# A mixture-of-experts stage whose TensorE order is written out by hand

## The chip, the cores and the metric

The kernel runs on one core of a Trainium2 chip. The metric is the device time of one execution in microseconds (us). TensorE is PE (PEld its weight loads), VectorE DVE, ScalarE ACT, GpSimd POOL, and SyncE, which issues the loads, SP.

## The reference, cut to what matters

Two layers of a diffusion transformer over 256 tokens of width 1024. Each layer mixes tokens (convolution, gated delta rule, windowed attention) and then channels. The second layer's channel mixer, the last stage of the kernel, is a mixture of eight experts, two for each token:

```python
top_logit, top_e = lax.top_k(logits, TOP_K)          # TOP_K = 2
gates = jax.nn.softmax(top_logit, axis=-1)
...
xb = h[row_tok]                                      # the tokens of each expert
y  = (silu(xb @ w_gate[e]) * (xb @ w_up[e])) @ w_down[e]     # 1024 -> 3584 -> 1024
out = segment_sum(y * row_gate, row_tok)
```

All is float32. `h` is the normalized x, scaled and shifted by a modulation.

## The kernel before

The change touches the routine `lean`, which runs when the experts' token counts fit fixed capacities: CAPS = [64, 96, 64, 160, 64, 96, 96, 32] tokens, the experts sorted so that the counts fit; this is the branch that runs. The other branch (`SEQ`) is not executed.

**Units and slots.** Each expert's 3584 inner columns are seven units of 512 (q = 0 to 6). A unit has three slots: gate (k = 0), up (k = 1) and down (k = 2). The matrix part of a slot is 2 MB, in four loads of 512 KB. `UNITS` lists experts 0, 1, 2 and 5 one after the other, then 3 and 7 alternating by q, then 6 and 4. `LEAN` lists the slots in the order of the program. With b the next unit and a the one before it, that order is gate(b), down(a), up(b).

**Loads.** The loads go into a ring of 36 buffers named r (nine slots), all issued by SP at L1186 (`ring_load`) in the order of the slots; load u waits until PE is done with load u - 36.

**Three ways of multiplying.** For 64 or 32 tokens (kind "f") PE does float32 matmuls, with tokens in parts of the columns of the array: L1535 for gate and up, L1769 for down. For 96 tokens (kind "t"), L1649 and L1652, and L1681 and L1684. Expert 3 has 160 tokens, a block of 128 (kind "s") and a rest of 32 (kind "f"). In the block of 128 each piece of weights, 128 x 512, is split in two parts, whi by ACT (L1499) and wlo = r - whi by DVE, or by POOL for every fourth piece (L1501, `wpiece`; four buffers of whi, three of wlo), and three matmuls use them (`three`, L1507 to L1509); the third, on wlo, is held back until after the first two of the next piece. A slot of that block has eight pieces.

**Between up and down.** `act` is Silu by ACT (L1729) and the product with up by DVE (L1730). `turn` transposes the result on PE (L1738; L1662 for 96 tokens) and copies it to hT, of which there is one buffer (DVE, L1745), or for expert 3 splits it into hr (ACT, L437) and hl (DVE, L438). The inner function `late` calls the former unit's turn in the middle of a gate.

**Gather, scatter, combine.** `lean_gather` brings the tokens of the next experts together: a one-hot matrix oe (DVE, L1614), products with the tokens on PE (L1623, two matmuls each, shown as four records), and a modulation out of PSUM by ACT (L433) or DVE (L431). It is a generator: each `next(steps)` in the program does one bank of PSUM. `BATCHES` says where it starts: experts 1 and 2 (width 160) and 5 and 4 (160), then 3, 7 and 6 (288). Expert 0 (width 64) is gathered ahead of the stage. `scatter` makes the matrix that puts an expert's rows back: DVE writes two halves into a buffer of hT (L1446), PE transposes them (L1450), ACT copies them (L1452). At q = 6 the results are copied to ys (`lean_rows`, L1696) and multiplied by the scatter matrix (`lean_combine`, L1717).

**What sets the order.** The program is written in the order above, but a scheduler of the framework decides the order of instructions on every engine, PE's too, by its own estimates of when operands are ready. PSUM has eight banks: four of tag x (gate, up, turn, gather, scatter, combine) and four of tag y (down).

Of the kernel before, what the change touches and what calls it, by code (L numbers as in the profile page):

```python
# [22 lines left out]
KT = 8  # L23
# [144 lines left out]
class Build:  # L168
# [995 lines left out]
    def ring_fill(self, n):  # L1164

        for _ in range(n):
# [4 lines left out]
    SEQ = [(0, 0), (1, 0)] + [t for q in range(6) for t in ((0, q + 1), (2, q), (1, q + 1))] + [(2, 6)]  # L1171
# [3 lines left out]
            + [(u[0], k, u[1]) for a, b in zip(UNITS, UNITS[1:]) for k, u in ((0, b), (2, a), (1, b))]  # L1175
# [195 lines left out]
    def expert(self, e, blocks):  # L1371
# [13 lines left out]
        hs, up, tr = {}, {}, {}  # L1385
        self.rest = None
        ahead = self.gather(e + 1) if e + 1 < NE else iter(())
        for j, (k, q) in enumerate(self.SEQ):
# [14 lines left out]
            else:  # L1403
                if q == 6:
                    next(ahead, None)
                for bi in order:
                    if bi in hs:
                        tr[bi] = self.turn(hs[bi], blocks[bi][2])
                if q == 6:
                    next(ahead, None)  # L1410
                for bi in order:
                    self.down(w, tr[bi], blocks[bi][1], blocks[bi][2], q, py[bi])
# [105 lines left out]
    def up(self, w, x, m, split, late):  # L1518

        nc = self.nc  # L1520
        if split:
            out = self.ps()
            for k in range(KT):
                if k == 4:
                    late()
# [5 lines left out]
        for k in range(KT):  # L1531
            if k == 4:
                late()
# [6 lines left out]
    def lean(self, first):  # L1540
# [5 lines left out]
        up = {}  # L1546
        for i, (e, k, q) in enumerate(self.LEAN):
            if (e, k, q) in self.BATCHES:
                got, steps = self.lean_gather(*self.BATCHES[e, k, q])
                xs.update(got)  # L1550
            w, x = self.slot(i), xs[e]
            bl = x["blocks"]
            if k == 0:
# [6 lines left out]
                up = [self.lean_up(w, b, late if b is bl[-1] else lambda: None) for b in bl]  # L1560
            elif k == 1:
                pu = [self.lean_up(w, b, lambda: None) for b in bl]
                pend = x, [self.act(g, u) for g, u in zip(up, pu)]
                if done:
                    self.lean_combine(done)
                    done = None
                if q == 6:
                    x["ogt"] = [self.scatter(e, s0, m, j) for j, (s0, m, _, _) in enumerate(bl)]
                next(steps, None)
            else:  # L1570
                if q == 0:
                    x["py"] = [[self.ps("y") for _ in range(1 if kind == "f" else 2)] for _, _, kind, _ in bl]
                if pend:
                    late()
                for b, h, py in zip(bl, x["tr"], x["py"]):
                    self.lean_down(w, h, b, q, py)
                if q == 6:
# [58 lines left out]
    def lean_up(self, w, b, late):  # L1636
# [7 lines left out]
        for k in range(KT):  # L1644
            if k == 4:
                late()
# [141 lines left out]
```

## Time and profile before

| | us |
|---|---|
| median of 3 runs | 2047.6 (2046.55 to 2048.73) |
| the profiled execution, its own time | 2046.76 |
| its span in the profile | 2045.0 |
| PE busy | 1942.6 (95%) |
| DVE, ACT, POOL busy | 930.4, 580.7, 237.8 |

The stage of the experts begins with the first L1535 at 1147 us of the span and fills the rest. A row of the timeline has the start, the duration, the engine, the line, the operation, the tiles (written <- read), the shapes and the number of instructions that the row groups, and in brackets the idle time ahead of it and what ended it. An L1535, L1769, L1623 or L1738 of the program shows as two records each.

### The profile page before, as it was taken

What the parts mean: (1) busy time and instruction counts of PE and PEld (TensorE: products, weight loads), DVE (VectorE), ACT (ScalarE), POOL (GpSimd) and SP (SyncE); (2) the same over time, 40 slices, a digit from 0 to 9 for tenths busy, and PEclk for the clock granted to TensorE, in tenths of its full rate; (3) what the DMA queues carried; (4) which work ended last, traced back from release to release, by engine and by line L of the source; (5) the groups of instructions that cost most, each with busy time, mean ns of one, the idle gap of its engine ahead of it and who ended that gap; (6) DMA issues with size and microseconds to landing.
All of it is one profiled execution on the core that took longest, in us unless ns stands there. A gap on an engine that the chain in (4) does not pass through costs nothing. (4 is left out here: it accounts for less than half of the span.)

```text
span 2045.0 us, 42975 instructions
## 1 busy us (share of the span) xinstructions
PE 1942.6 (95%) x17677; PEld 1474.0 (72%) x17677; DVE 930.4 (45%) x1858; ACT 580.7 (28%) x1079; POOL 237.8 (12%) x378
## 2 busy tenths in 40 slices
PE   6998999989999999887999899999999999999996
PEld 4776777668888887767878558875788766569853
DVE  4687666787645534587667111110113544430012
ACT  3732224452222223633225100000012444410001
POOL 1165100010000000063400000000001222200000
PEclk9999999999999999899999799999999999999998
DMA  7544452145445423245107899999999999989993
GB/s 302 162 90 113 143 200 100 52 168 191 147 168 202 164 73 106 80 105 123 40 22 276 312 409 408 408 406 409 402 399 408 407 391 376 347 306 397 378 398 150
DMA packets 186544, 497.79 MB, mean 243 GB/s; under 512 B 64865, under 2 KB 83425, under 8 KB 173793
## 3 DMA queue, kind: packets, MB, share of 16 engines
q1 hardware_dynamic: 186336, 494.94, 65.8%
q8 instruction: 141, 2.31, 0.5%
q14 instruction: 67, 0.54, 0.1%
HBM read 485.96 MB, written 8.91 MB: 242 GB/s over the span
## 5 line engine op out<-in xcount | busy, mean ns | idle before, releaser
L437 ACT ACTIVATE wh<-w 128x1024 fp32r<-128x1024 f32 (+4 forms) x162 | 141.6, 887 | 378.7 <-PE psx L467 195.2
L1649 PE MATMUL psx<-r,Xb 128*32 128x384 f32 x2016 | 231.8, 488 | 0.1
L1652 PE MATMUL psx<-r,Xb 128*32 128x128 f32 x2016 | 231.4, 273 | 0.0
L1652 PEld LDWEIGHTS psx<-r,Xb 128*32 128x32 f32 x2016 | 216.2, 110 | 1.1
L438 DVE TENSOR_TENSOR wl<-w,wh 128x1024 fp32r<-128x1024 f32 (+4 forms) x162 | 162.9, 1014 | 116.9 <-ACT wh L437 116.4
L1730 DVE TENSOR_TENSOR hm<-hm,psx 128x256 f32<-128x256 f32 (+3 forms) x63 | 29.3, 465 | 387.2 <-PE psx L1652 197.3
L1729 ACT ACTIVATE hm<-psx 128x256 f32<-128x256 f32 (+3 forms) x63 | 26.4, 418 | 441.1 <-PE psx L1652 227.1
L466 PE MATMUL psx<-xh,wh 128*128 128x512 f32 (+1 forms) x384 | 137.4, 386 | 11.1 <-ACT xh L437 8.1
L466 PE MATMUL psx<-fxh,wh 128*128 128x512 f32 x352 | 138.2, 394 | 5.0 <-ACT fxh L437 5.0
L468 PE MATMUL psx<-xh,wl 128*128 128x512 f32 (+1 forms) x384 | 131.7, 373 | 8.0 <-DVE wl L438 8.0
L1535 PE MATMUL psx<-r,Xb 128*64 128x256 f32 (+1 forms) x1792 | 137.8, 328 | 0.0
L467 PE MATMUL psx<-fxl,wh 128*128 128x512 f32 x352 | 137.4, 390 | 0.0
L468 PE MATMUL psx<-fxh,wl 128*128 128x512 f32 x352 | 137.3, 390 | 0.0
L467 PE MATMUL psx<-xl,wh 128*128 128x512 f32 (+1 forms) x384 | 132.9, 374 | 0.7 <-DVE xl L438 0.7
L1501 POOL TENSOR_TENSOR wlo<-r,whi 128x512 fp32r<-128x512 f32 x42 | 57.3, 1365 | 609.9 <-ACT whi L1499 448.1
L1501 DVE TENSOR_TENSOR wlo<-r,whi 128x512 fp32r<-128x512 f32 x126 | 97.6, 788 | 63.4 <-PE psx L1509 25.6
L1535 PEld LDWEIGHTS psx<-r,Xb 128*64 128x64 f32 (+1 forms) x1792 | 88.8, 123 | 43.6 <-issue 13.2
L1499 ACT ACTIVATE whi<-r 128x512 fp32r<-128x512 f32 x168 | 99.3, 627 | 47.4 <-DVE wlo L1501 15.8
L1684 PE MATMUL psy<-r,hT 128*32 128x256 f32 (+1 forms) x672 | 112.7, 326 | 0.0
L1681 PE MATMUL psy<-r,hT 128*32 128x384 f32 x1008 | 112.1, 486 | 0.0
L1769 PE MATMUL psy<-r,hT 128*32 128x256 f32 (+1 forms) x784 | 111.5, 473 | 0.5 <-DVE hT L1745 0.5
L466 PEld LDWEIGHTS psx<-xh,wh 128*128 128x128 f32 x384 | 74.1, 199 | 27.9 <-ACT xh L437 9.0
(402 smaller groups left out, 3622.8 us busy)
## 6 DMA issues: line engine op xcount, KB each, us to landing
r<-mg SPq DMA_DIRECT2D x224, 512.0 KB, 10.1
r<-mu SPq DMA_DIRECT2D x224, 512.0 KB, 10.1
r<-md SPq DMA_DIRECT2D x224, 512.0 KB, 10.1
wm<-wmod SPq DMA_DIRECT2D x32, 1024.0 KB, 6.5
w<-win SPq DMA_DIRECT2D x24, 1024.0 KB, 5.2
w<-wgu SPq DMA_DIRECT2D x22, 1024.0 KB, 5.0
w<-wmod SPq DMA_DIRECT2D x16, 1024.0 KB, 6.8
w<-wdn SPq DMA_DIRECT2D x16, 704.0 KB, 4.0
```

The source lines that it names most:

```text
L437: nc.scalar.activation(hi, src, AF.Copy)
L438: nc.vector.tensor_tensor(lo, src, hi.bitcast(F), op=OP.subtract)
L466: nc.tensor.matmul(out, wh[:, k, :], xh[:, k, :n], start=start and k == 0, stop=False)
L467: nc.tensor.matmul(out, wh[:, k, :], xl[:, k, :n], start=False, stop=False)
L468: nc.tensor.matmul(out, wl[:, k, :], xh[:, k, :n], start=False, stop=stop and k == kn - 1)
L1501: eng.tensor_tensor(wl, src, wh.bitcast(F), op=OP.subtract)
L1535: nc.tensor.matmul(out[m * j:m * j + m, :], x[:, k, :], w[k // 2][:, k % 2 * 512 + j * fw:k % 2 * 512 + (j + 1) * fw], start=k == 0, stop= ...
L1649: nc.tensor.matmul(out[32 * g:32 * g + 32], x[:, k, 32 * g:32 * g + 32], w[k // 2][:, c:c + 384], start=k == 0, stop=k == KT - 1, skip_gro ...
L1652: nc.tensor.matmul(out[96:, g * P:(g + 1) * P], x[:, k, 32 * g:32 * g + 32], w[k // 2][:, c + 384:c + 512], start=k == 0 and g == 0, stop= ...
L1681: nc.tensor.matmul(py[half][32 * g:32 * g + 32, :384], lhs[g], w[ft][:, 384 * half:384 * half + 384], start=first, stop=last, skip_group_c ...
L1684: nc.tensor.matmul(py[half][96:, o:o + n], lhs[g], w[ft][:, 768 + c:768 + c + n], start=first and o == 0, stop=last, skip_group_check=True)
L1769: nc.tensor.matmul(py[0][m * dq:m * dq + m, :dw], lhs, w[ft][:, dq * dw:(dq + 1) * dw], start=q == 0 and ft == 0, stop=q == 6 and ft == 3, ...
```

## The change

- PE's instructions of the whole stage keep the order of the program: `manual_schedule` for PE alone. The other engines are ordered by the scheduler as before.
- That program order is a new one: gate(b), up(b), down(a).
- `late`, the turn of the former unit, stands at the third product of up's first block (k == 2), where it stood at the fifth of the last block of gate.
- `scatter` stands behind the down of q = 5, where it stood behind the up of q = 6. The combine of an expert stands behind the next unit's down, not its up.
- The gather does two steps behind each down, where it did one behind each up and each down. A step does all its products first, then all modulations; a bank holds at most four products. So the first gather (expert 0) fills two banks of four, the first modulated by ACT, the second by DVE; before, it was one bank, product and modulation by turns. The batch of experts 1 and 2 starts one unit earlier.

```diff
--- before.py
+++ after.py
@@ -1168,11 +1168,11 @@
                 self.ring_load(self.loaded)
                 self.loaded += 1
 
-    SEQ = [(0, 0), (1, 0)] + [t for q in range(6) for t in ((0, q + 1), (2, q), (1, q + 1))] + [(2, 6)]
+    SEQ = [(0, 0), (1, 0)] + [t for q in range(6) for t in ((0, q + 1), (1, q + 1), (2, q))] + [(2, 6)]
     UNITS = ([(e, q) for e in (0, 1, 2, 5) for q in range(7)] + [(e, q) for q in range(7) for e in (3, 7)]
              + [(e, q) for e in (6, 4) for q in range(7)])
     LEAN = ([(0, 0, 0), (0, 1, 0)]
-            + [(u[0], k, u[1]) for a, b in zip(UNITS, UNITS[1:]) for k, u in ((0, b), (2, a), (1, b))]
+            + [(u[0], k, u[1]) for a, b in zip(UNITS, UNITS[1:]) for k, u in ((0, b), (1, b), (2, a))]
             + [(UNITS[-1][0], 2, 6)])
 
     def ring_load(self, u):
...
@@ -1521,7 +1521,7 @@
         if split:
             out = self.ps()
             for k in range(KT):
-                if k == 4:
+                if k == 2:
                     late()
                 self.three(out, [x[0][:, k], x[1][:, k]], self.wpiece(w, k), k == 0, k == KT - 1)
             return out
@@ -1529,7 +1529,7 @@
         fw = 512 // ct
         out = self.ps()[:, :fw]
         for k in range(KT):
-            if k == 4:
+            if k == 2:
                 late()
             for j in range(ct):
                 nc.tensor.matmul(out[m * j:m * j + m, :], x[:, k, :],
@@ -1543,47 +1543,50 @@
 
         xs, pend, done, steps = dict(first), None, None, iter(())
         self.rest = None
-        up = {}
-        for i, (e, k, q) in enumerate(self.LEAN):
-            if (e, k, q) in self.BATCHES:
-                got, steps = self.lean_gather(*self.BATCHES[e, k, q])
-                xs.update(got)
-            w, x = self.slot(i), xs[e]
-            bl = x["blocks"]
-            if k == 0:
+        up = []
+        with self.tc.manual_schedule(engines={mybir.EngineType.PE}):
+            for i, (e, k, q) in enumerate(self.LEAN):
+                if (e, k, q) in self.BATCHES:
+                    got, steps = self.lean_gather(*self.BATCHES[e, k, q])
+                    xs.update(got)
+                w, x = self.slot(i), xs[e]
+                bl = x["blocks"]
+
                 def late():
                     nonlocal pend
                     if pend:
                         x0, hs = pend
                         x0["tr"] = [self.lean_turn(h, b[2]) for h, b in zip(hs, x0["blocks"])]
                         pend = None
-                up = [self.lean_up(w, b, late if b is bl[-1] else lambda: None) for b in bl]
-            elif k == 1:
-                pu = [self.lean_up(w, b, lambda: None) for b in bl]
-                pend = x, [self.act(g, u) for g, u in zip(up, pu)]
-                if done:
-                    self.lean_combine(done)
-                    done = None
-                if q == 6:
-                    x["ogt"] = [self.scatter(e, s0, m, j) for j, (s0, m, _, _) in enumerate(bl)]
-                next(steps, None)
-            else:
-                if q == 0:
-                    x["py"] = [[self.ps("y") for _ in range(1 if kind == "f" else 2)] for _, _, kind, _ in bl]
-                if pend:
-                    late()
-                for b, h, py in zip(bl, x["tr"], x["py"]):
-                    self.lean_down(w, h, b, q, py)
-                if q == 6:
-                    self.lean_rows(x)
-                    done = x
+
+                if k == 0:
+                    up = [self.lean_up(w, b, lambda: None) for b in bl]
+                elif k == 1:
+                    pu = [self.lean_up(w, b, late if b is bl[0] else lambda: None) for b in bl]
+                    pend = x, [self.act(g, u) for g, u in zip(up, pu)]
                 else:
-                    next(steps, None)
-            for u in range(4 * i, 4 * i + 4):
-                self.ring_load(u + len(self.ring))
-        self.lean_combine(done)
-
-    BATCHES = {(0, 2, 2): (1, 2), (1, 2, 1): (5, 4), (5, 2, 0): (3, 7, 6)}
+                    if q == 0:
+                        x["py"] = [[self.ps("y") for _ in range(1 if kind == "f" else 2)] for _, _, kind, _ in bl]
+                    if (e, q) == self.UNITS[-1]:
+                        late()
+                    for b, h, py in zip(bl, x["tr"], x["py"]):
+                        self.lean_down(w, h, b, q, py)
+                    if done:
+                        self.lean_combine(done)
+                        done = None
+                    else:
+                        for _ in range(2):
+                            next(steps, None)
+                    if q == 5:
+                        x["ogt"] = [self.scatter(e, s0, m, j) for j, (s0, m, _, _) in enumerate(bl)]
+                    if q == 6:
+                        self.lean_rows(x)
+                        done = x
+                for u in range(4 * i, 4 * i + 4):
+                    self.ring_load(u + len(self.ring))
+            self.lean_combine(done)
+
+    BATCHES = {(0, 2, 1): (1, 2), (1, 2, 1): (5, 4), (5, 2, 0): (3, 7, 6)}
 
     def lean_gather(self, *es):
 
@@ -1614,15 +1617,15 @@
                     nc.vector.tensor_scalar(oe[:, b, o:o + m], self.M["iota"][:, :m], self.pos[:, b, e:e + 1],
                                             self.r[:, b:b + 1], op0=OP.is_equal, op1=OP.mult)
             yield
-            per = min(KT, 512 // width)
+            per = min(KT // 2, 512 // width)
             for k0 in range(0, KT, per):
-                px = self.ps()
-                for k in range(k0, min(k0 + per, KT)):
-                    c = (k - k0) * width
+                px, v = self.ps(), k0 // per % 2
+                ks = [(k, (k - k0) * width) for k in range(k0, min(k0 + per, KT))]
+                for k, c in ks:
                     for b in range(2):
                         nc.tensor.matmul(px[:, c:c + width], self.xtok[:, b, k * P:(k + 1) * P], oe[:, b, :width],
                                          start=b == 0, stop=b == 1)
-                    v = k0 // per % 2
+                for k, c in ks:
                     if first:
                         hm = self.mt.tile([P, 512], F, name="hm", bufs=2)[:, :P]
                         self.modulate(1, 3, k, 0, hm, px[:, c:c + P], v)
@@ -1642,7 +1645,7 @@
             return self.up(w, x, m, kind == "s", late)
         out = self.ps()[:, :384]
         for k in range(KT):
-            if k == 4:
+            if k == 2:
                 late()
             c = k % 2 * 512
             for g in range(3):
```

What the change does to the order of PE's instructions is seen in three places (x4: four instructions; r_8904 is a ring buffer, Xb and X_9750 hold gathered tokens). First, the gather for experts 1 and 2, in the third unit of expert 0 of the kernel before:

```order
L1535 MATMUL psx<-r_8903,X_9750 64x256 x4
L1623 MATMUL psx<-oe,xtok 128x160 x2
L1535 MATMUL psx<-r_8904,X_9750 64x256 x3
L1623 MATMUL psx<-oe,xtok 128x160 x2
L1535 MATMUL psx<-r_8904,X_9750 64x256
L1535 MATMUL psx<-r_8905,X_9750 64x256 x3
L1623 MATMUL psx<-oe,xtok 128x160 x2
L1535 MATMUL psx<-r_8905,X_9750 64x256
```

and with the change, where the second step is the last row's ten:

```order
L1772 MATMUL psy<-r_9667,hT 64x512 x2
L1626 MATMUL psx<-oe,xtok 128x160 x6
L1535 MATMUL psx<-r_9668,X_9750 64x256 x4
...
L1772 MATMUL psy<-r_8903,hT 64x512 x2
L1626 MATMUL psx<-oe,xtok 128x160 x10
```

Single products between the matmuls of a gate became two runs behind a down. Second, expert 3 after its first pair of units, a gate of the kernel before:

```order
L1509 MATMUL psx<-wlo,X 128x512
L1535 MATMUL psx<-r_9449,Xr 32x128 x3
L1535 MATMUL psx<-r_9450,Xr 32x128
L1507 MATMUL psx<-whi,X 128x512
L1508 MATMUL psx<-whi,X 128x512
L1509 MATMUL psx<-wlo,X 128x512
L1507 MATMUL psx<-whi,X 128x512
L1508 MATMUL psx<-whi,X 128x512
L1509 MATMUL psx<-wlo,X 128x512
L1535 MATMUL psx<-r_9450,Xr 32x128 x4
```

and with the change the end of such a gate:

```order
L1507 MATMUL psx<-whi,X 128x512
L1508 MATMUL psx<-whi,X 128x512
L1509 MATMUL psx<-wlo,X 128x512 x2
L1535 MATMUL psx<-r_8904,Xr 32x128 x8
L1535 MATMUL psx<-r_8905,Xr 32x128 x8
L1535 MATMUL psx<-r_8906,Xr 32x128 x8
L1535 MATMUL psx<-r_8907,Xr 32x128 x8
```

The rest's 32 matmuls stood in fours between every two pieces, and now stand behind all eight pieces. Third, the scatter's transposes (L1450) of expert 0, before:

```order
L1769 MATMUL psy<-r_8899,hT 64x512 x2
L1535 MATMUL psx<-r_8900,X_9750 64x256 x4
L1535 MATMUL psx<-r_8901,X_9750 64x256 x4
L1535 MATMUL psx<-r_8902,X_9750 64x256 x4
L1535 MATMUL psx<-r_8903,X_9750 64x256 x4
L1450 MATMUL psx<-cnorm,hT 128x128 x2
```

and with the change:

```order
L1772 MATMUL psy<-r_8901,hT 64x512 x2
L1772 MATMUL psy<-r_8902,hT 64x512 x2
L1772 MATMUL psy<-r_8903,hT 64x512 x2
L1450 MATMUL psx<-cnorm,hT 128x128 x2
L1652 MATMUL psx<-r_8904,Xb 32x384 x3
```

A whole up stood between the last reader of hT and the transposes; now they follow that reader directly.

## Rows read from the trace of the kernel before

**Rows 1.** Busy time by stretch: us, each engine's busy time, PEclk, DMA share, GB/s.
```profile
1150.00:1447.00 297.00, 296.90 (x3259) 204.21 (x3257) 34.48 (x84) 18.12 (x39) 0.00 (x0) 1.00 1.02 402
...
1650.00:2012.00 362.00, 358.10 (x4360) 249.42 (x4362) 100.76 (x171) 78.37 (x145) 35.62 (x27) 1.00 0.98 368
```

**Rows 2.** Timeline: loads issued by SP, and PE's first use of the slot.
```profile
1426.96 4.51 SPq L1186 DMA_DIRECT2D r<-md  x4
...
1443.78 1.51 PE L1769 MATMUL psy<-r,hT 128*64 128x512 f32 x6
...
1997.75 4.16 SPq L1186 DMA_DIRECT2D r<-md  x4
...
2021.59 3.65 PE L1769 MATMUL psy<-r,hT 128*64 128x512 f32 x16 [0.51 <-DVE hT L1745]
```

**Rows 3.** The page's DMA issues: KB each, median us from issue to landing.
```profile
r<-md SPq DMA_DIRECT2D x224, 512.0 KB, 10.1
```

**Rows 4.** Timeline of the first gather and the stage's start.
```profile
1134.85 1.09 PE L1623 MATMUL psx<-oe,xtok 128*128 128x64 f32 x4 [1.88 <-DVE oe L1614]
...
1136.43 0.93 PEld L1623 LDWEIGHTS psx<-oe,xtok 128*128 128x128 f32 x4 [0.68 <-ACT X L433]
1136.43 1.12 PE L1623 MATMUL psx<-oe,xtok 128*128 128x64 f32 x4 [0.49 <-ACT X L433]
...
1147.16 5.08 PE L1535 MATMUL psx<-r,X 128*64 128x256 f32 x24
...
1149.17 2.03 SPq L1186 DMA_DIRECT2D r<-md  x2
```

**Rows 5.** Timeline of the gather for experts 1 and 2.
```profile
1185.51 3.62 PE L1535 MATMUL psx<-r,X 128*64 128x256 f32 x32
1189.07 0.81 PE L1623 MATMUL psx<-oe,xtok 128*128 128x160 f32 x4
...
1190.81 0.57 PEld L1623 LDWEIGHTS psx<-oe,xtok 128*128 128x128 f32 x4 [0.38 <-ACT Xb L433]
...
1192.57 0.81 PE L1623 MATMUL psx<-oe,xtok 128*128 128x160 f32 x4
```

**Rows 6.** Timeline of ACT: the split of expert 3's h, once a pair.
```profile
1590.95 0.60 ACT L437 ACTIVATE hr<-psx 128x512 fp32r<-128x512 f32 x1 [7.00 <-PE psx L1738]
...
1620.98 0.60 ACT L437 ACTIVATE hr<-psx 128x512 fp32r<-128x512 f32 x1 [4.80 <-PE psx L1738]
...
1798.28 0.60 ACT L437 ACTIVATE hr<-psx 128x512 fp32r<-128x512 f32 x1 [1.21 <-PE psx L1738]
```

**Rows 7.** Timeline of expert 3: pieces on PE, and their differences on DVE.
```profile
1591.96 0.50 PE L1507 MATMUL psy<-whi,hr 128*128 128x512 f32 x1
...
1597.55 1.93 PE L1769 MATMUL psy<-r,hT 128*32 128x256 f32 x32
1599.30 1.93 PE L1535 MATMUL psx<-r,Xb 128*32 128x128 f32 x64
...
1624.27 2.08 DVE L1501 TENSOR_TENSOR wlo<-r,whi 128x512 fp32r<-128x512 f32 x3 [1.69 <-issue]
...
1627.00 1.21 DVE L1501 TENSOR_TENSOR wlo<-r,whi 128x512 fp32r<-128x512 f32 x1 [0.66 <-PE psy L1509]
...
1634.67 0.50 PE L1507 MATMUL psx<-whi,X 128*128 128x512 f32 x1
...
1636.61 0.50 PE L1507 MATMUL psx<-whi,X 128*128 128x512 f32 x1
```

**Rows 8.** Timeline: the scatter's two halves on DVE, expert 3.
```profile
1809.60 0.60 DVE L1446 TENSOR_SCALAR hT<-ckeep,pos,gate 128x128 f32<-128x128 f32 x2 [2.69 <-PE psx L1535]
```

**Rows 9.** Groups by line, 1680 to 1780 us: busy us, mean ns, idle before.
```profile
L1499 ACT ACTIVATE whi<-r 128x512 fp32r<-128x512 f32 x68 | 40.4, 627 | 23.0 <-DVE wlo L1501 11.9 <-PE psx L1508 5.0 <-PE psy L1508 4.9
L1501 DVE TENSOR_TENSOR wlo<-r,whi 128x512 fp32r<-128x512 f32 x52 | 40.2, 787 | 27.2 <-PE psx L1509 15.2 <-ACT whi L1499 7.5 <-PE psy L1509 4.3
L1501 POOL TENSOR_TENSOR wlo<-r,whi 128x512 fp32r<-128x512 f32 x18 | 24.3, 1352 | 81.3 <-ACT whi L1499 22.6 <-PE psx L1509 15.6 <-PE psy L1507 14.6
```

More of the change, by code (lines that the diff above doesn't have):

```diff
@@ L1406, in expert @@
                 for bi in order:
-                    if bi in hs:
-                        tr[bi] = self.turn(hs[bi], blocks[bi][2])
+                    if bi not in tr:
+                        tr[bi] = self.turn(hs.pop(bi), blocks[bi][2])
                 if q == 6:
@@ L1411, in expert @@
                 for bi in order:
-                    self.down(w, tr[bi], blocks[bi][1], blocks[bi][2], q, py[bi])
+                    self.down(w, tr.pop(bi), blocks[bi][1], blocks[bi][2], q, py[bi])
                 if q == 6:
```

## The prediction

> **What bounds the kernel now.** I read the busy times by stretch first. From 1150 us on the core does one thing: it multiplies the experts' matrices, 672 loads of 512 KB, as they pass through a ring of 36 buffers. [rows 1] gives PE 296.90 of 297 us in the first stretch, with the DMA engines full as well (share 1.02, 402 GB/s). In the second, 1650 to 2012 us, PE is busy 358.10 of 362 us, and the rate is down to 368 GB/s. So early on PE and the loads are level, and later PE holds the loads up. The timeline says how level: the four loads issued from 1426.96 on take 4.51 us to issue, a load lands 10.1 us after its issue (median), and PE uses the first of them at 1443.78 [rows 2, 3]. The last of the four lands at about 1426.96 + 4.51 + 10.1 = 1441.6, 2 us before PE comes to that matrix's first use: the smallest lead of the whole stage. The last four, issued from 1997.75, have landed by 1997.75 + 4.16 + 10.1 = 2012.0, and are used from 2021.59: a lead of 9.6 us.
>
> So a microsecond taken from PE after 1150 us is a microsecond of the time as long as the loads keep ahead. But "busy" hides a waste: matmuls of different kinds that alternate cost more than the same ones in one run, and the record counts the whole as busy. That is where I looked next.
>
> **The change, part by part.**
>
> *First gather (expert 0, ahead of the stage).* [rows 4] shows a ping-pong: four PE records (two matmuls) for one product, then ACT's modulation out of the same bank, then the next product 1.58 us after the one before (1134.85 to 1136.43). Eight rounds fill 1134.85 to 1147.16, 12.3 us. Now four products go into a bank before its first modulation, and the next four into another. The idle 0.49 us of seven rounds, 3.4 us, is the least that goes. If products follow each other as the four weight loads of one do (0.93 us), it is 12.3 - 8 x 0.93 = 4.9. I take **-4.6 us**, near the upper end, since the 1.12 us of a round holds the pipeline's emptying, which a row of products has once. SP's first load of the stage, at 1149.17, waits for PE to have used up the first four buffers, so the loads' start moves forward by the same amount.
>
> *Later gathers (experts 1 and 2; 5 and 4; 3, 7 and 6).* Two are of width 160 and eight products each, one of width 288 and eight: 24 products, each wedged singly between matmuls of an expert. [rows 5]: from the wedge at 1189.07 to the one two further on, at 1192.57, there are 3.50 us, with two wedges and seven L1535 in between (three and four by the order of the program, 14 records). The unbroken run at 1185.51 has 3.62 / 32 = 0.113 us a record; the four weight loads of a wedge follow each other in 0.57 us, which I take as its price among its like. 2 x 0.57 + 14 x 0.113 = 2.72, so a wedge wastes (3.50 - 2.72) / 2 = 0.39 us: 24 x 0.39 = **-9.4 us** (0 if the modulations now make the next step's bank late; -13 if the eight wide products waste twice 0.39).
>
> *Experts 3 and 7.* This is the main term. Expert 3's block of 128 tokens is done in pieces of 512 columns, three matmuls each, 24 pieces to a pair of units (3, q) and (7, q). The split of h by ACT happens once in a pair and serves as a clock [rows 6]: 1590.95 to 1620.98 is 30.03 us, but from there to 1798.28 five pairs take 177.30, 35.46 each. The first pair is laid out as the change lays out all. In [rows 7] the eight pieces of its down run from 1591.96 to the next kind at 1597.55, 5.59 us or 0.70 a piece. Later the scheduler puts eight records of the 32-token rest between every two pieces, and 1634.67 to 1636.61 is 1.94 us for two pieces and eight such records; a run of 64 records of that size takes 1.93 us in the first pair, eight of them 0.24, so two pieces in a run and eight records in a run would be 2 x 0.70 + 0.24 = 1.64. The fixed order puts pieces in runs of eight again. If each pair then takes 30.03, six intervals fall from 207.33 to 180.18 us: **-27.2 us**. The last down of expert 3, behind 1798.28, is a third of a pair's pieces: (35.46 - 30.03) / 3 = **-1.8 us**. In the other direction the change puts two piece runs (gate, up) directly behind the down's run, with only some 2 us of the rest between, where the first pair had 4; the bound of that stands under the rivals.
>
> *Scatter matrices.* They move from the up of q = 6, where the scheduler slid their transposes among other matmuls, to a fixed place behind the down of q = 5. They use the one buffer hT, which the down reads to its end. So PE now stands while DVE writes both halves, 0.60 us for two [rows 8], and the crossing to PE. The crossing is at most the 0.51 us that PE shows ahead of the last down [rows 2]; between 0.6 and 1.1 us, I take 0.85, nine times: **+7.6 us** (5.4 to 9.9). Behind it waits only PE's next gate, nothing of SP's.
>
> *The rest.* The combines stand behind a down, whole; before, some were wedged between L1535 groups: -1 us (0 to -2, three to five such wedges at 0.39). The very last down follows its own up at once in the kernel before, with 0.51 us idle at the head [rows 2] and as much before the turn; now the former unit's down lies between: -0.6 us. The turn of h at product 2 of up, not 4 of gate, and gate-up-down for gate-down-up, cost nothing: the product of Silu and up has a whole down, over 3 us, to be done in. The tail behind the last down stays.
>
> *Do the loads follow?* Before 1447 us PE gains 16 x 0.39 = 6.2 from two gathers and loses 3 x 0.85 to scatters: 3.7 net, and the lead there is 2 us (the start comes earlier for both alike). So PE now waits for loads there, **+1.7 us**. Behind it, 362 us at 368 GB/s are 133 MB; at 402 they take 331, 31 us less. With the start, the last load can land 31 + 4.6 = 35.6 us earlier, at 1976, and PE could begin the last down 35.6 + 9.6 = 45 us earlier. It comes 35 earlier. So the loads still lead at the end, by some 10 us.
>
> The sum: -4.6 - 9.4 - 27.2 - 1.8 + 7.6 - 1.0 - 0.6 + 1.7 = -35.3. The profiled execution took 2046.8 us, 0.8 under the median of the runs, less than the runs differ by, and left aside: 2046.8 - 35.3 = **2011.5 us**.
>
> **The rivals.**
>
> 1. *The loads become the bound.* If the pairs fall below 30 us, or the gathers give more, PE catches up with the loads at the end: no earlier than 2046.8 - 45 = 2002. For it: the lead of 2 us at 1443.78. Against: 10 us of room. 2000 to 2006.
> 2. *The splits pace the pieces.* A piece needs ACT's copy (627 ns), and DVE's difference, or POOL's for every fourth (787 and 1352 ns, [rows 9]). Alone, DVE does one in 2.08 / 3 = 0.69 us, but 1.21 beside POOL [rows 7]: the two exclude each other. If so throughout, four pieces cost 3 x 0.69 + 1.35 = 3.42 us, 0.86 a piece; in a pair 24 x (0.86 - 0.70) = 3.8 us of the 5.4 are lost again, 23 in six pairs, and the time is about 2035. For it: gate's and up's runs now stand closer together. Against: up to three pieces are split ahead, and in the first pair eight pieces took 5.59 with POOL at work. Half of that loss gives 2023. The Trainium skill, page "SBUF — State Buffer", section "Who interferes with whom", has the same exclusion as a rule, for a DVE instruction with two SBUF inputs against a GpSimd one that reads SBUF; the 1.21 us agrees.
> 3. *Slower: PE stands at each piece.* The scheduler's filling covered waits for the splits; in a fixed order nothing fills them. The rest of a pair is 30.03 - 24 x 0.70 = 13.2 us, so a pair is as slow as now when a piece costs (35.46 - 13.2) / 24 = 0.93 us. If copy and difference do not overlap, a piece costs 0.63 + 0.79 = 1.42; halfway between, 1.17, a pair takes 41.3, and six cost +35 instead of -27: 2011.5 + 62 = 2074. Against: PE's 5.59 for eight.
> 4. *The loads go no faster than now.* If 368 GB/s is the loads' own limit there, and not PE's holding them up, PE gains only what it can draw from the lead and the start: 2046.8 - 9.6 - 4.6 = 2032.6. Against: 402 GB/s over 297 us of this very stage [rows 1]. The Trainium skill, page "DMA: Bandwidth & Descriptors", section "Where 436 GB/s comes from", is for it: of transfers from HBM to SBUF it says that the HBM side, about 358 GB/s a core, is what binds. The 402 GB/s lie above that figure, so the trace does not agree, and the measurement decides.
> 5. *The pairs don't change*, since something else set their 35.46: 2011.5 + 29 = 2041.
>
> **How the numbers follow.** Forecast, PE bound with pairs of 30 to 31 us, 2004 to 2020: 0.60. Rival 1: 0.11. Rival 2, 2020 to 2038: 0.17 (two thirds of it under 2030). Rival 3: 0.06. Rival 4: 0.02. Rival 5: 0.04, of which 0.03 within 0.2% of the time before. The range of 2001 to 2030 leaves out the tail of rival 2, rivals 3 to 5, and the lower edge of rival 1, under 0.2 together. A measurement of this kernel can tell about 0.2%, 4 us, from no change; so faster 0.91, same 0.03, slower 0.06.
>
> **What would show it.** First L1535 at about 1142.6 instead of 1147.16 and SP's next load with it. Splits of h 30 to 31 us apart in all seven pairs. Pieces 0.23 us a matmul in runs of eight, with no gap at L1509 (a gap there, released by POOL or DVE, is rival 2 or 3). The scatter's transposes with 0.6 to 1.1 us idle ahead, nine times. 1650 to 1950 at over 385 GB/s, and the last load landed some 5 to 10 us before its use. The forecast is wrong if PE shows idle time released by r (rival 1), or if the pairs differ from 30 by more than 2.

## The result, and the profile after

The changed kernel takes 2014.5 us (median of 4 runs, 2013.63 to 2015.93) against 2047.6: a ratio of 0.9837, 95% interval 0.9823 to 0.9852. The forecast was 2011.5 us, range 2001 to 2030. The profiled execution has a span of 2013.5 us against 2045.0.

What precedes the first gather is the same program in every kernel here, but its end moves by some microseconds from profile to profile (PE's first gather matmul at 1134.85 before, 1135.69 after). So below I compare the **stage**: from that matmul to the end of the span. It is 2045.0 - 1134.85 = 910.2 us before and 2013.5 - 1135.69 = 877.8 after: **-32.3 us**. The forecast's terms add up to -35.3.

The first gather and the start, on the timeline of the changed kernel (to be read beside [rows 4]):

```profile
1135.69 7.06 PE L1626 MATMUL psx<-oe,xtok 128*128 128x64 f32 x32 [1.88 <-DVE oe L1617]
1139.37 1.29 ACT L433 ACTIVATE X<-psx,mod 128x64 f32<-128x64 f32 x4 [5.95 <-PE psx L1626]
1142.68 3.50 PE L1535 MATMUL psx<-r,X 128*64 128x256 f32 x16
1144.69 0.33 SPq L1186 DMA_DIRECT2D r<-mu  x1
```

All 32 records run through in 6.99 us (12.31 before), and ACT modulates four products in one go beside PE. SP's next load follows the first use by the same 2.0 us as before.

Busy time by stretch, the same columns as [rows 1]:

```profile
1143.00:1440.00 297.00, 294.88 (x3355) 207.94 (x3351) 36.33 (x93) 17.53 (x39) 0.00 (x0) 1.00 1.01 400
...
1640.00:1980.00 340.00, 331.25 (x4308) 248.79 (x4301) 101.77 (x167) 77.54 (x145) 35.57 (x26) 1.00 1.01 399
```

The loads go on at 399 GB/s where they had fallen to 368. PE, which was busy 98.9% of that stretch, is busy 97.4% of the new one: it works less and stands more. What it stands for, by the view of waits (PE alone, 1143 to 1994 us: us in total, times, longest):

```profile
PE psy L1509 <- DVE wlo L1501: 4.4, 6, 0.9
PE psx L1450 <- DVE hT L1446: 3.9, 8, 0.5
...
PE psx L1535 <- issue: 1.7, 3, 0.7
...
PE psy L1772 <- DMA r<-md: 0.8, 4, 0.2
...
PE psx L1652 <- DMA r<-mg: 0.3, 1, 0.3
```

The first row is new and was not in the forecast's sum (it is the sign that the forecast named for rivals 2 and 3); the second is the scatter; the last two are loads, 1.1 us in all. The view has one more row, three stops of 1.7 us in all at L1535 in expert 7's gate or up, marked "issue": PE stands there for nothing that the profile shows.

The pace of experts 3 and 7, by the split of h on ACT's timeline. First two more rows of the kernel before, to be read with [rows 6]:

```profile
1654.49 0.60 ACT L437 ACTIVATE hr<-psx 128x512 fp32r<-128x512 f32 x1 [6.41 <-PE psx L1738]
...
1760.20 0.60 ACT L437 ACTIVATE hr<-psx 128x512 fp32r<-128x512 f32 x1 [6.42 <-PE psx L1738]
```

The six old intervals are 30.03, 33.51, three of 35.2, and 38.08 us. The changed kernel:

```profile
1577.74 0.60 ACT L437 ACTIVATE hr<-psx 128x512 fp32r<-128x512 f32 x1 [1.13 <-PE psx L1741]
...
1611.83 0.60 ACT L437 ACTIVATE hr<-psx 128x512 fp32r<-128x512 f32 x1 [10.29 <-PE psx L1741]
...
1643.71 0.60 ACT L437 ACTIVATE hr<-psx 128x512 fp32r<-128x512 f32 x1 [10.20 <-PE psx L1741]
...
1674.56 0.60 ACT L437 ACTIVATE hr<-psx 128x512 fp32r<-128x512 f32 x1 [9.19 <-PE psx L1741]
...
1736.33 0.60 ACT L437 ACTIVATE hr<-psx 128x512 fp32r<-128x512 f32 x1 [9.19 <-PE psx L1741]
...
1771.05 0.60 ACT L437 ACTIVATE hr<-psx 128x512 fp32r<-128x512 f32 x1 [10.48 <-PE psx L1741]
```

The six new intervals are 34.09, 31.88, three of 30.85 to 30.90, and 34.72 us: 193.31 in all, against 207.33 before and 180.18 in the forecast. The three in the middle are undisturbed pairs: 30.87 us, not 35.2, and not 30.03. The first interval now holds the combine of expert 5 and the last a third scatter matrix, which lay outside the six before; the stops marked "issue" fall near the ends of the first and second and in the last. What is left over in an undisturbed pair is seen in the down of one such pair, on the timeline of PE, DVE and POOL:

```profile
1676.42 4.44 DVE L1501 TENSOR_TENSOR wlo<-r,whi 128x512 fp32r<-128x512 f32 x5
...
1676.96 1.29 POOL L1501 TENSOR_TENSOR wlo<-r,whi 128x512 fp32r<-128x512 f32 x1 [9.91 <-ACT whi L1499]
1677.16 0.50 PE L1509 MATMUL psy<-wlo,hr 128*128 128x512 f32 x1
...
1678.86 0.50 PE L1509 MATMUL psy<-wlo,hr 128*128 128x512 f32 x1 [0.74 <-DVE wlo L1501]
...
1689.99 1.04 PE L1509 MATMUL psx<-wlo,X 128*128 128x512 f32 x2
```

DVE begins the first difference at 1676.42 and is free for the second at 1677.1, but POOL has begun the third piece's at 1676.96 and ends at 1678.25. Five differences of 0.69 us would be 3.45 us; they take 4.44. PE stands 0.74 us for the second. At the end of the gate's run the last two L1509 hold PE until 1690.97, 0.98 us where two matmuls take 0.46.

The scatter, on the timeline of expert 0:

```profile
1217.95 3.60 PE L1772 MATMUL psy<-r,hT 128*64 128x512 f32 x16
...
1221.63 0.60 DVE L1446 TENSOR_SCALAR hT<-ckeep,pos,gate 128x128 f32<-128x128 f32 x2 [2.94 <-PE psy L1772]
...
1222.03 0.58 PE L1450 MATMUL psx<-cnorm,hT 128*128 128x128 f32 x2 [0.48 <-DVE hT L1446]
```

DVE writes the two halves one after the other, and PE begins with the first half 0.40 us after DVE began: it stands 0.48 us, not 0.85. The eight such waits of the stage are 0.44 to 0.55 us each, and the ninth scatter, expert 5's, shows none.

The last loads (timeline, beside [rows 2]):

```profile
1960.22 9.16 SPq L1186 DMA_DIRECT2D r<-md  x8
...
1990.18 3.65 PE L1772 MATMUL psy<-r,hT 128*64 128x512 f32 x16 [0.52 <-DVE hT L1748]
```

With 10.1 us to landing they are there by 1979.5: a lead of 10.7 us at the end, as forecast.

### The profile page after: what moved, and what is told of

Its sections match the earlier page's. It is cut to its first block, busy times and chain, and to the rows that moved or that the text cites. A ratio compares the mean times of both kernels' runs of the same rounds, so it can differ in the third digit from the quotient of the medians.

```text
span 2013.5 us, 42986 instructions
## 1 busy us (share of the span) xinstructions
PE 1907.0 (95%) x17677; PEld 1476.4 (73%) x17677; DVE 936.7 (47%) x1862; ACT 577.4 (29%) x1075; POOL 236.7 (12%) x378
## 5 line engine op out<-in xcount | busy, mean ns | idle before, releaser
L1652 PE MATMUL psx<-r,Xb 128*32 128x384 f32 x2016 | 225.0, 487 | 1.4 <-DVE xs L1072 0.9
L1535 PE MATMUL psx<-r,Xb 128*64 128x256 f32 (+1 forms) x1792 | 130.9, 327 | 1.7 <-issue 1.7
L1501 DVE TENSOR_TENSOR wlo<-r,whi 128x512 fp32r<-128x512 f32 x126 | 104.2, 857 | 44.0 <-ACT whi L1499 32.5
L1535 PEld LDWEIGHTS psx<-r,Xb 128*64 128x64 f32 (+1 forms) x1792 | 87.3, 123 | 41.6 <-issue 8.4
L1687 PE MATMUL psy<-r,hT 128*32 128x256 f32 (+1 forms) x672 | 112.7, 326 | 0.0
L1772 PE MATMUL psy<-r,hT 128*32 128x256 f32 (+1 forms) x784 | 104.1, 472 | 1.5 <-DMA r<-md 0.8
## 6 DMA issues: line engine op xcount, KB each, us to landing
r<-mg SPq DMA_DIRECT2D x224, 512.0 KB, 10.1
r<-mu SPq DMA_DIRECT2D x224, 512.0 KB, 10.1
r<-md SPq DMA_DIRECT2D x224, 512.0 KB, 10.1
```

Of the source, the lines that this page charges most:

```text
L1501: eng.tensor_tensor(wl, src, wh.bitcast(F), op=OP.subtract)
L1535: nc.tensor.matmul(out[m * j:m * j + m, :], x[:, k, :], w[k // 2][:, k % 2 * 512 + j * fw:k % 2 * 512 + (j + 1) * fw], start=k == 0, stop= ...
L1652: nc.tensor.matmul(out[32 * g:32 * g + 32], x[:, k, 32 * g:32 * g + 32], w[k // 2][:, c:c + 384], start=k == 0, stop=k == KT - 1, skip_gro ...
L1687: nc.tensor.matmul(py[half][96:, o:o + n], lhs[g], w[ft][:, 768 + c:768 + c + n], start=first and o == 0, stop=last, skip_group_check=True)
L1772: nc.tensor.matmul(py[0][m * dq:m * dq + m, :dw], lhs, w[ft][:, dq * dw:(dq + 1) * dw], start=q == 0 and ft == 0, stop=q == 6 and ft == 3, ...
```

## The experiments

For each: the median and the ratio to the kernel before, measured beside it, and the stage as defined above (910.2 before, 877.8 changed). The stage comes from one profile of each kernel. "Pairs" are the undisturbed ones. Where the text speaks of PE's time for some instructions, it is the sum over the stage of their waits and of the time from each one's start to the next one's start or wait; the products of experts 3 and 7 (gate, up and down) so take 231.9 us before and 212.7 changed.

**1. Only the fixed order.** The kernel before, with

```diff
+        with self.tc.manual_schedule(engines={mybir.EngineType.PE}):
             for i, (e, k, q) in enumerate(self.LEAN):
```

> The kernel before, with nothing changed but that PE keeps the order of its own old program (gate, down, up; old places of turn, scatter and combine; old gather). Theory (expert 3's pairs were long because other matmuls stood between its pieces): the pairs fall from 35.4 to 30 to 31 us, about -20 us in all. But the old gather, product and modulation by turns in one bank, can no longer be filled with matmuls of an expert, and each of 24 products costs PE a wait of about 1.2 us instead of 0.39: +19. So 2040 to 2052 us, with the pairs at 31. Rival (the new slot order and places are what pays): pairs stay at 34 or more, time over 2060.

Measured: 2031.7 us, ratio 0.9913 (0.9896 to 0.9929); stage 896.4, **-13.7**. The pairs are 31.66 us, close to the theory's 30 to 31 and not the rival's 34 or more, and the products of experts 3 and 7 take 213.2 us: nearly all that the change gains on them comes with the fixed order alone. The time lies below the 2040 to 2052 that was expected, since the price of the old gather in a fixed order was put far too high.

Part of this profile runs at a lower clock than the two it is compared with. Columns as in [rows 1]; PEclk, the granted clock, is the third number from the end:

```profile
1780.00:1795.30 15.30, 14.93 (x166) 9.62 (x166) 7.06 (x12) 6.55 (x13) 2.78 (x2) 1.00 0.98 375
1795.50:1812.40 16.90, 16.90 (x71) 9.03 (x69) 3.28 (x8) 0.38 (x1) 0.00 (x0) 0.50 0.45 169
```

From 1795.5 us on, within expert 3's combine, TensorE ran at the lower of its two levels (1.2 instead of 2.4 GHz) for 17 us, though PE had been busy for 14.93 of the 15.3 us before. The changed kernel and the one before did this combine at 1.00. Half of 17 us, some 8 us, is the estimated cost, so at the full clock the stage would be some 22 us shorter than before, not 13.7. The times agree: the run with the highest mean clock (0.973) took 2026.3 us, the three others (0.969 and 0.970) 2031.5 to 2032.0. The profiles of experiments 2 and 4 have 6.8 us of the same kind at the same place, some 3.4 us of cost each; why the clock fell in these three is open.

The pairs of experiment 1 lose 0.96 us at the head of each down, on the timeline of ACT, DVE and PE:

```profile
1713.63 0.60 ACT L437 ACTIVATE hr<-psx 128x512 fp32r<-128x512 f32 x1 [6.16 <-PE psx L1739]
...
1714.83 0.28 ACT L1730 ACTIVATE hm<-psx 128x128 f32<-128x128 f32 x1 [0.60 <-PE psx L1535]
1715.00 4.38 ACT L1499 ACTIVATE whi<-r 128x512 fp32r<-128x512 f32 x8
...
1715.68 0.50 PE L1507 MATMUL psy<-whi,hr 128*128 128x512 f32 x1 [0.96 <-ACT whi L1499]
```

In ACT's queue expert 7's Silu stands between the split of h and the copies. It waits 0.60 us for expert 7's gate to end, and PE's next piece waits behind it.

**2. Only the gather.** The kernel before with the new steps:

```diff
-            per = min(KT, 512 // width)
+            per = min(KT // 2, 512 // width)
...
+                for k, c in ks:
```

> The kernel before, scheduler and all, with the new gather steps alone (products of a bank first, then its modulations; at most four to a bank). Theory: the first gather ends 4.5 us earlier and the loads start as much earlier; of the later wedges some join up; the pairs of experts 3 and 7 stay at 35.4 us. 2038 to 2043 us. Rival (the gather is the larger part of the gain): under 2030.

Measured: 2036.9 us, 0.9944 (0.9927 to 0.9960), a little below the expected range; stage 903.1, **-7.1**, in a profile of the slowest of the four runs (2042.0 us). Pairs of 35.2 us, as before. The first gather is 5.3 of the 7.1. Without the stretch at the lower clock the 7.1 would be some 10.5, so the later gathers, with what they disturb, give an estimated 5 even under the scheduler.

**3. The changed kernel with the old gather.** The inverse edit.

> The changed kernel with the old gather steps (one product, then its modulation, then the next product in the same bank). Theory: the first gather costs its 4.5 us again, and in the fixed order each of the 24 later products makes PE wait for a modulation, about 1.2 us: +20 to +33 over the changed kernel, 2035 to 2048 us, with the pairs still at 30.9. Rival (the later gathers matter little, since loads bound the early experts anyway): 2019 us.

Measured: 2031.4 us, 0.9924 (0.9907 to 0.9940); stage 891.2, **+13.4** over the changed kernel, 5.3 of it the first gather and 8.1 the others. The theory's direction held, its size did not (+20 to +33). PE's timeline shows why:

```profile
1193.86 0.81 PE L1626 MATMUL psx<-oe,xtok 128*128 128x160 f32 x4
1195.21 0.81 PE L1626 MATMUL psx<-oe,xtok 128*128 128x160 f32 x4 [0.54 <-DVE Xb L431]
```

A product comes 1.35 us after the one before in its bank, against 0.58 in a row (five products in 2.91 us in the changed kernel), and the first of a bank waits for nothing.

**4. The rest between the pieces again.** The changed kernel; in gate and up of expert 3:

```diff
                 self.three(out, [x[0][:, k], x[1][:, k]], self.wpiece(w, k), k == 0, k == KT - 1)
+                if rest and k % 2:
+                    next(rest, None)
```

where `rest` issues the 32-token block's four matmuls of one k.

> The changed kernel, in which four matmuls of expert 3's 32-token rest stand behind every second piece in gate and up, as the scheduler had put them before; order fixed, nothing else changed. Theory (changing between the two kinds costs PE): eight places in a pair at 0.30 us each, pairs at 33.3 instead of 30.9 us, six to seven pairs: 2028 to 2032 us. Rival (the old pairs were long for waits on the splits, and the rest between was free filling): pairs at 31 or less, 2014 us.

Measured: 2024.4 us, 0.9890 (0.9874 to 0.9907); stage 888.5, **+10.7**, of which some 3.4 are the lower clock; the products of experts 3 and 7 take 220.3 us, 7.6 more than in the changed kernel. Pairs of 32.3 us, 1.4 more, between theory and rival. PE's timeline around one place:

```profile
1688.10 0.39 PE L1509 MATMUL psx<-wlo,X 128*128 128x512 f32 x1
1688.42 0.43 PE L1651 MATMUL psx<-r,Xr 128*32 128x128 f32 x8
1688.78 0.50 PE L1507 MATMUL psx<-whi,X 128*128 128x512 f32 x1
1689.11 0.39 PE L1508 MATMUL psx<-whi,X 128*128 128x512 f32 x1
```

From 1688.10 to 1689.11 are 1.01 us for two matmuls of 0.23 and eight records of 0.03: 0.31 us are the change of kind, as the forecast's rows said. Eight such places would be 2.5 us; 1.1 come back, most of it at the ends of the two runs, where the last two L1509 take 0.55 us in this kernel and 0.98 in the changed one: the rest between the pieces covers waits for the splits. Rival: refuted, but its idea, that filling covers waits, is a part of it.

**5. A buffer for the scatter.** The changed kernel, with

```diff
+        if e in (3, 7):
+            og = self.mt.tile([P, 512], F, name="hT", bufs=1)[:, :N]
+        else:
+            og = self.mt.tile([P, 512], F, name="hm", bufs=2)[:, :N]
```

> The changed kernel, whose scatter matrices of experts other than 3 and 7 are written into a buffer of hm, which is free at that time, instead of the one hT that the down reads to its end. Theory: PE no longer stands 0.5 us ahead of six of the nine pairs of transposes; three of the six lie where the loads bound the time, so only some 1.5 us of 3 show: 2011.5 to 2014 us. Rival (the 0.85 us a scatter of the prediction): -5, 2009.5 us.

Measured: 2014.0 us (2011.48 to 2016.8), 0.9838 (0.9825 to 0.9852); stage 876.2, **-1.6**. The time cannot tell it from no change, and the stage does not bear the theory out either. PE's waits ahead of the transposes are, with the new buffer:

```profile
PE psx L1453 <- DVE hm L1449: 1.7, 1, 1.7
PE psx L1453 <- DVE hT L1449: 1.5, 3, 0.5
```

That is 3.2 us where the changed kernel has 3.9: five waits of 0.5 us are gone, but a new one of 1.7 us stands in expert 5, for DVE's write into hm, so the buffer was not free in time there. Most of the rest of the 1.6 is L1509's waits (3.4 us in five against 4.4 in six), which the edit does not touch.

**6 and 7. POOL.** The changed kernel, with POOL for the seventh piece alone in the downs:

```diff
-        eng = self.nc.gpsimd if i % 4 == 2 else self.nc.vector
+        eng = self.nc.gpsimd if i % 4 == 2 and i > first else self.nc.vector
```

(`first` is 2 in `down`, 0 elsewhere), and with no POOL at all:

```diff
-        eng = self.nc.gpsimd if i % 4 == 2 else self.nc.vector
+        eng = self.nc.vector
```

> The changed kernel; in expert 3's downs POOL makes the difference of the seventh piece alone, no longer that of the third. Theory (POOL's instruction shuts DVE out; DVE's second difference stands behind POOL's and PE waits 0.74 us for it, once in each of seven downs): the gap goes, pairs fall from 30.9 to 30.1 us, 2009 to 2010 us. Rival (the gap is the chain from the split of h through ACT's copies, whoever makes the differences): 2014.5 us, the gap stays.

> The changed kernel with all differences on DVE, none on POOL. Theory (POOL's help costs DVE about what it saves): DVE needs 24 x 0.69 = 16.6 us of a pair's 30; no gap in the down: 2009 to 2010 us. Rival (DVE at 0.69 us a piece cannot keep ahead of PE at 0.69 us a piece within a run of eight): gaps at the ends of the runs, pairs of 32 us or more, over 2020 us.

Measured: 2009.6 us, 0.9811 (0.9798 to 0.9824), stage 872.8, **-5.0**, pairs of 29.9; and **2005.5 us**, 0.9784 (0.9771 to 0.9798), stage 866.3, **-11.5**, pairs of 29.1. Both theories hold, the second beyond its number. DVE and POOL in a down on the timeline of the kernel with POOL late:

```profile
1674.06 3.69 DVE L1501 TENSOR_TENSOR wlo<-r,whi 128x512 fp32r<-128x512 f32 x6
...
1677.61 1.31 POOL L1501 TENSOR_TENSOR wlo<-r,whi 128x512 fp32r<-128x512 f32 x1 [12.93 <-PE psy L1509]
...
1678.14 2.52 DVE L1501 TENSOR_TENSOR wlo<-r,whi 128x512 fp32r<-128x512 f32 x3 [0.40 <-ACT whi L1499]
```

and DVE and PE in a down and the gate behind it, on the timeline of the kernel without POOL:

```profile
1675.49 4.33 DVE L1501 TENSOR_TENSOR wlo<-r,whi 128x512 fp32r<-128x512 f32 x7
...
1681.87 6.08 DVE L1501 TENSOR_TENSOR wlo<-r,whi 128x512 fp32r<-128x512 f32 x9 [2.05 <-PE psy L1509]
...
1686.16 0.61 PE L1509 MATMUL psx<-wlo,X 128*128 128x512 f32 x2
1686.70 1.52 PE L1535 MATMUL psx<-r,Xr 128*32 128x128 f32 x48
```

Six differences in 3.69 us while POOL rests, three in 2.52 beside it; without it nine in 6.08. The run's last two L1509 fall from 0.98 to 0.54 us. POOL cost PE 1.8 us a pair, and 11.0 us over the products of experts 3 and 7 (201.7 us without it). The Trainium skill, page "SBUF — State Buffer", section "Who interferes with whom", states the exclusion of a DVE instruction with two SBUF inputs and a GpSimd one that reads SBUF; these rows agree.

**8. The old order of slots, and 10. the turn late.** The changed kernel with gate, down, up and the turn at the fifth product of the last block of gate:

```diff
-            + [(u[0], k, u[1]) for a, b in zip(UNITS, UNITS[1:]) for k, u in ((0, b), (1, b), (2, a))]
+            + [(u[0], k, u[1]) for a, b in zip(UNITS, UNITS[1:]) for k, u in ((0, b), (2, a), (1, b))]
...
-                    up = [self.lean_up(w, b, lambda: None) for b in bl]
+                    up = [self.lean_up(w, b, late if b is bl[-1] else lambda: None) for b in bl]
...
-            if k == 2:
+            if k == 4:
```

and the changed kernel with the last change (k == 4) alone, which in both leaves expert 3's own block of 128 as it was.

> The changed kernel with the old order of slots (gate of the next unit, down of the former, up of the next) and the turn at its old place (fifth product of the last block of the next gate), still in a fixed order. Theory of the prediction (slot order and place of the turn cost nothing): within 3 us of the changed kernel, 2012 to 2017 us. Rival (behind an up the chain of Silu, product, transposes and copy has only half a gate for cover, and PE stands in each unit of a fixed order): 0.2 to 0.5 us in each of 56 units, 2025 to 2040 us.

> The changed kernel with the turn of h at the fifth product of up, no longer at the third; slot order and all else as changed. Theory (the split of h, a Silu and the first copy of a piece, 0.60 + 0.27 + 0.55 us and crossings on ACT, lie between the turn and expert 3's down; half an up, 1.0 us, covers less of it than three quarters, 1.5 us): PE stands some 0.5 us more in each of seven downs, pairs of 31.2 to 31.6 us, 2016 to 2020 us. Rival (the place costs nothing, as predicted, and the 0.8 us a pair of the old slot order come from the order): pairs of 30.9 us, 2014.5 us.

Measured: the old order 2020.4 us, 0.9866 (0.9851 to 0.9881), stage 882.5, **+4.7**, pairs of 31.6; the late turn 2017.4 us (2014.34 to 2018.98), 0.9858 (0.9842 to 0.9874; it overlaps the changed kernel's), stage 876.1, **-1.7** (what precedes the stage took 4.2 us longer in this profile), pairs of 30.4. The old order lies between its theory (up to 2017) and its rival (from 2025). It puts expert 7's gate directly ahead of the down, and with it the Silu in ACT's queue that was seen in experiment 1 (0.97 us on L1507, again); with gate, up, down that gate is long done. So in the pairs it is the order, not the place of the turn. But of the 4.7 us in the stage only half can be the order's: 2.3 us lie behind the last combine, where DVE begins a reciprocal after 5.29 us of idle time instead of 2.92, 1.2 are longer waits at the scatter and 1.2 the turns. The products of experts 3 and 7 take 212.3 us, no more than the 212.7 of the changed kernel: what the later pairs lose, the first ones win back, which have no stop marked "issue" here and no wait at the second L1509. The theory of the late turn is wrong: PE waits 0.25 us for the first copy there, but the second L1509 of the down loses less.

**9. Both improvements.** No POOL, and the scatter's buffer.

> All differences on DVE, and the scatter's own buffer: the two edits that shortened PE's part of the changed kernel, by 11.5 and 1.6 us from the first gather to the end. Theory (without POOL the loads run at 404 GB/s from the stage's start to its end and land 3 us before their use, so they bound the time): PE's gain is lost to waits for r, 2003 to 2006 us, no more than 2 us below the kernel without POOL. Rival (PE still bounds): the 1.6 us come off in full and PE shows no more waits for loads than there.

Measured: 2005.6 us (2003.48 to 2008.87), 0.9807 (0.9793 to 0.9821); stage 867.3, **+1.0** over the kernel without POOL. No gain, as the theory said. The loads run at 405 GB/s from 1150 to 1975 us, and at the end they lead by nothing that matters:

```profile
1959.60 9.26 SPq L1186 DMA_DIRECT2D r<-md  x8
...
1979.67 3.65 PE L1775 MATMUL psy<-r,hT 128*64 128x512 f32 x16 [0.52 <-DVE hT L1751]
```

With 10.1 us to landing they are there by 1979.0, 0.7 us ahead of their use (10.7 in the changed kernel; 0.3 in the one without POOL, by the same count). PE waits for r at the end of expert 2 (waits of PE and of its weight loads, 1146 to 2000 us):

```profile
PE psy L1775 <- DMA r<-md: 2.1, 3, 1.6
...
PEld psy L1775 <- DMA r<-md: 5.2, 5, 2.5
```

The kernel without POOL has 0.9 and 4.4 us in these rows. Behind the longest wait, 1.6 us, the granted clock is 0.50 for 3.4 us:

```profile
1425.90 3.59 PE L1775 MATMUL psy<-r,hT 128*64 128x512 f32 x8 [0.20 <-DMA r<-md]
```

Eight records take the time of sixteen, 1.8 us more than at the full clock. So what is gained ahead of that place is lost there. The scatter's new wait of 1.7 us is in this kernel too. This also weighs the figure for loads once more (the Trainium skill, page "DMA: Bandwidth & Descriptors", section "Where 436 GB/s comes from", about 358 GB/s a core): 405 GB/s over 825 us, by one core alone, lie above it, so the trace does not agree.

## Why the prediction was right, and where a size was off

- **What bounds the kernel**: right. PE's time beyond 1150 us was the time, and the loads followed, at 399 instead of 368 GB/s, with 10.7 us of lead at the end (forecast: some 10). The 2 us of lead at 1443 were used up and PE waited 1.1 us for r, all between 1424 and 1444 us; forecast 1.7.
- **First gather**: forecast -4.6, measured 12.31 - 6.99 = -5.3. The upper end, 4.9, was taken from four weight loads of 0.93 us; in a row of 32 records a product takes 6.99 / 8 = 0.87.
- **Experts 3 and 7**: the mechanism was right, and fixing the order alone brought it (experiment 1). The size was not: their products give 19.2 us (231.9 to 212.7), where -27.2 - 1.8 = -29.0 was forecast. The step that failed is "if each pair then takes 30.03", set against 35.46 for each of the old pairs. The undisturbed pairs take 30.87, 0.84 us more. The first pair's row did not show a down whose first pieces are still to be split when it begins. That is rival 2 in part (0.17 in the forecast): DVE's second difference stands behind POOL's, 0.74 us once in each down. The row with the exclusion, 1.21 us [rows 7], stood in the forecast, but was taken to be covered by pieces split ahead. And the old pairs were not all of 35.46: that is a mean of 33.51, three of 35.2, and 38.08, the last with two scatter matrices in it. In the new kernel, too, the first, second and last interval are longer than the undisturbed ones, in part by work that moved into them. So the sign "30 to 31 us apart in all seven pairs" held in three of six intervals.
- The price of the old pairs was put down to changes of kind alone. They cost 0.3 us a place, as [rows 7] gave it; but experiment 4 shows that eight places add 1.4 us net, not 2.4. Waits were in the old pairs too: the view of PE's waits before has 2.8 us on ACT's copies.
- **Scatter**: forecast +7.6, measured +4.0 (3.9 to 7.9 us of PE's time), with eight waits of 0.44 to 0.55 us. The term counted both halves of DVE's write; PE needs the first to begin.
- **Slot order and place of the turn** "cost nothing": the place of the turn does not. The order saves 0.8 us in an undisturbed pair, since it takes a Silu that would wait out of ACT's queue, but nothing over all products of experts 3 and 7, and at most 2.4 us in the stage (experiment 8).
- **Later gathers**: -9.4 in the forecast. In a fixed order the old steps cost 8.1 us more than the new ones, and under the scheduler the new steps give an estimated 5. Their gain against the wedges of before was not isolated.
- The whole stage by PE's time in us, each instruction with its own waits:

| | before | changed | change | forecast |
|---|---|---|---|---|
| first gather | 12.3 | 7.0 | -5.3 | -4.6 |
| products of experts 3 and 7 | 231.9 | 212.7 | -19.2 | -29.0 |
| scatter | 3.9 | 7.9 | +4.0 | +7.6 |
| later gathers, combines, products of the other experts, waits for loads | 619.7 | 609.5 | -10.2 | -9.4 - 1.0 + 1.7 |
| turns, with the last down's wait in the forecast | 25.4 | 23.9 | -1.5 | -0.6 |
| behind the last combine | 17.0 | 17.0 | 0.0 | 0.0 |

- That the sum came within 3 us is in part luck: the pairs gave 9.8 us less than forecast, and the other rows 6.7 more.
- The rivals: 3 (PE stands at each piece) and 5 (pairs don't change) did not come. 4 (loads at 368) is refuted. 1 (the loads as the bound) becomes true only for the kernels without POOL, at 2005.5 us, near the 2002 given for it: there the loads' lead at the end is 0.3 and 0.7 us.

## What to carry to other kernels

An engine that is 99% busy can still waste time in changes between kinds of matmul; compare a stretch where the kinds stand in runs with one where they alternate. A fixed order takes that waste away but shows every wait that filling had covered: read the in-order queues that feed the engine, for a waiting instruction that stands ahead of the one you need (a Silu ahead of a copy). And a second engine that helps is no help if it shuts the first one out: try the work on one engine alone. And before you take the difference of two profiles, compare their granted clocks stretch by stretch: in experiment 1 the clock hid some 8 of 22 us.

## What the runs showed of the hardware that was not expected

DVE alone did all 168 differences faster for PE than DVE with POOL for a quarter of them: 29.1 us a pair against 30.9. Nine in a row took 6.08 us, 0.68 each, and kept ahead of PE, which uses one in 0.68 us (three matmuls at 0.227), although DVE had no margin within a run.

The granted clock was 0.50 in the middle of the stage, for 17 us in experiment 1 and 6.8 us in experiments 2 and 4, though PE was busy; the changed kernel and the one before did the same combine at 1.00.
